# Two expert streams: steps of wide and narrow experts alternate instead of whole experts in turn

## The chip, the cores and the metric

The kernel runs on one core of one Trainium2 chip. The metric is the device time of one execution in microseconds, the median over runs. Arrays are float32; the kernel works on 256 tokens of width 1024.

## The reference

Two layers, each a mixer and then a channel mixer. The first layer's channel mixer is a dense SwiGLU, the second a mixture of eight experts of which each token uses two. The change touches the second alone:

```python
def swiglu(h, w1, w3, w2):
    return (jax.nn.silu(h @ w1) * (h @ w3)) @ w2

def moe_swiglu(h, router_w, w1, w3, w2):
    logits = (h @ router_w).astype(jnp.float32)
    top_v, top_i = lax.top_k(logits, TOP_K)
    probs = jax.nn.softmax(top_v, axis=-1)
    gates = jnp.sum(jax.nn.one_hot(top_i, N_EXPERTS) * probs[..., None], axis=-2)
    y = jnp.zeros_like(h)
    for e in range(N_EXPERTS):
        y = y + gates[..., e:e + 1] * swiglu(h, w1[e], w3[e], w2[e])
    return y
```

Each expert has w1 and w3 of 1024 x 2816 and w2 of 2816 x 1024. After it come `x = x + gt_f * y` and a last RMSNorm with the gains `final_g`.

## The kernel before, in words

The weights of an expert come from HBM in 33 loads of 1 MB (tile `raw`, 128 x 2048): 22 of w1 and w3 (tensors in_m1, in_m3), 11 of w2 (in_m2). `load` (L128) issues them on SP's queue. A tile of `raw` belongs to a pool; in the expert stage there are eight such tiles in turn (`more` and `rawp`, L767 to L771) and, for the first thirteen loads alone, four of a pool `ahead` and one that shares the place of `xn`.

Experts are sorted by how many tokens chose them, into eight places. The even places have 128 slots and are called wide here, the odd ones 64 slots, called narrow. `place` (L843) makes that order on VectorE (DVE): it counts with a matmul, ranks, and writes `number_i`, the expert's number of each place. SP reads seven of these numbers into registers (`values_load`, L878), since a load of any place but the first has its address from such a register (`of_place`, L893). Place 0 is always expert 0.

`prepare` (L905) gathers the tokens of one or two places by matmuls with a one-hot matrix `oh` (tile `pm`, two PSUM banks) and writes `x_hi`, `x_lo` for a wide place (a float32 split into two float32r parts) or `x_n` for a narrow one.

`inner` (L1017) computes one of six column blocks c of w1 and w3; a block is four loads (two for c = 5). For a wide place each half of a load is split by `split` (L133): ScalarE (ACT) writes `whi`, DVE the rest `wlo`, with five pairs of buffers, and PE then takes three matmuls for each product (`mm3`, L152). For a narrow place (`inner_narrow`, L1000) PE multiplies `raw` as it is, in float32, w1 into partitions 0 to 63 and w3 into 64 to 127 of one bank; each such matmul stands as two records in the trace. A narrow block ends with a copy of that bank on ACT (L1014).

`turn` (L971) then transposes the block by four matmuls on PE into a bank `pm` and writes `a_hi`, `a_lo` (wide) or, through Silu on ACT, `a_n` (narrow). `outer` (L1048) multiplies by w2: two banks `pb` for a wide place, one for a narrow place. `scatter` (L1080) splits the result into `ob`, spreads it over the tokens by matmuls with `oht` (bank `pm`) and adds it times the token's gate to `y` on DVE.

The program goes through the places in order (L1117 to L1147): six blocks, then 11 loads of w2. The turn of block c stands behind the matmuls of block c + 1, the scatter of a place behind the first block of the next place. In the third block of the last place, `y` is multiplied by `gate_f` and added to `xs` (L1133, L1134), the gains are loaded over `y` (L1135) and scaled (L1137); the last place's scatter adds to `xs` directly. The queues of the engines are filled in an order that a scheduler finds at build time; each engine then works through its own in that order.

```python
            done = (e, outer(e))
        scatter(*done)
```

Of the kernel before, what the change touches and what calls it, by code (L numbers as in the profile page):

```python
# [17 lines left out]
P = 128  # L18
H = 64
# [18 lines left out]
HOLD_E = (0, 3, 2, 1)  # L38

# [19 lines left out]
def trunk(  # L59
# [49 lines left out]
    def const(shape, dt, name, pl=cst):  # L109
        return pl.tile(shape, dt, tag=name, name=name)  # L110
# [93 lines left out]
    ones = const([P, P], F32, "ones")  # L204
# [179 lines left out]
    def wide(tag):  # L384
        return cst.tile([P, KD, SEQ], F32R, tag=tag, name=nm(tag))
# [371 lines left out]
    def experts():  # L757
# [61 lines left out]
        iota_i = et([P, P], "iota_i", I32)  # L819
        pool.iota(iota_i[:], pattern=[[1, P]], base=1, channel_multiplier=0)  # L820
        iota = et([P, P], "iota")
        dve.tensor_copy(iota[:], iota_i[:])

        def turned(oh, dt):

            tp = pm()
            tv = tp[:, :SEQ].rearrange("p (t s) -> p t s", t=NT)
            for t in range(NT):
                transpose(tv[:, t, :], oh[:, t, :].bitcast(F32))
            o = et([P, NT, P], "oht", dt, bufs=3)  # L830
            act.activation(o[:], tv, AF.Copy)
            return o
# [10 lines left out]
        def place():  # L843
# [60 lines left out]

        def prepare(places):  # L905
# [18 lines left out]
            if e == 0:  # L924

                tn = cst.tile([P, NT, D], F32, tag="wide_lo", name="tn")
# [44 lines left out]
        def turn(p, c, a):  # L971
# [14 lines left out]
            if c == 0 and wide_place(p):  # L986
                for h in ("a_hi", "a_lo"):
                    aa[h] = aa["pool"].tile([P, KF, P], F32R, tag=h, name=nm(h))
            elif c == 0:
                aa["a_n"] = aa["pool"].tile([P, KF, H], F32, tag="a_lo", name=nm("a_n"))  # L990
            if not wide_place(p):
                g = wk.tile([P, 4, H], F32, tag="s", name=nm("g"))
# [55 lines left out]
        def outer(e):  # L1048
            if not wide_place(e):
                acc = pb()  # L1050
                for u in range(11):
# [8 lines left out]
            acc = [pb(), pb()]  # L1060
# [6 lines left out]
            for u in range(11):  # L1067
# [12 lines left out]
        def scatter(e, acc):  # L1080
# [17 lines left out]
            for c in range(2):  # L1098
                s = slice(c * 512, (c + 1) * 512)
                if wide_place(e):  # L1100
                    r = slice(0, P)
                    o_hi, o_lo = parts(c, acc[c][:], gate_f[:, s])
# [13 lines left out]

        prepare((0,))  # L1117
        done = None
        for e in range(NE):
            last = None  # L1120
            for c in range(6):
                a = inner(e, c)
                if c == 0 and done is not None:
                    scatter(*done)
                if last is not None:
                    turn(e, c - 1, last)
                last = a
                if c == 1 and e == 0:
                    place()
                if c == 2 and e == NE - 1:  # L1130
                    y = aa["y"]
                    for t in range(NT):
                        dve.tensor_tensor(y[:, t, :], y[:, t, :], gate_f[:], op=ALU.mult)  # L1133
                        dve.tensor_tensor(xs[:, t, :], xs[:, t, :], y[:, t, :], op=ALU.add)  # L1134
                    act.dma_start(y[:, 0, :], fg.to_broadcast([P, D]))  # L1135
                    fgt = y[:, 1, :]
                    act.activation(fgt, y[:, 0, :], AF.Copy, scale=32.0)  # L1137
                    gn = cst.tile([P, 512], F32, tag="wide_hi", name="gate_n")
                    for i in range(2):
                        r = slice(H * i, H * i + H)  # L1140
                        act.activation(gn[r], gate_f[r, i * 512:(i + 1) * 512], AF.Copy)
                    aa["gate_n"] = gn[:]
            turn(e, 5, last)
            if wide_place(e):
                prepare(tuple(p for p in (e + 1, e + 2) if p < NE))
            done = (e, outer(e))
        scatter(*done)  # L1147

        fin = cst.tile([P, NT, D], F32, tag="wide_lo", name="fin")
# [12 lines left out]
        with tc.If(flag > 0):  # L1162
            for e in range(NE):
# [3 lines left out]
                h = cst.tile([P, KD, P], F32, tag="wide_hi", name=nm("xo"))  # L1167
# [159 lines left out]
```

## Time and profile before

| | us |
|---|---|
| median of 3 runs | 1218.04 (1217.74 to 1220.62) |
| the profiled execution, its own time | 1221.47 |
| its span, first to last instruction | 1219.8 |
| TensorE (PE) busy | 1152.5 (94%) |
| DVE busy | 710.4 (58%) |
| ACT busy | 586.6 (48%) |

A span of 1219.8 us is cut into stages by the trace's time. The first matmul of an expert starts near 483 us, the last near 1201 us, so that the expert stage is 718 us of the span. In it SP issues 264 loads of 1 MB. PE's busy time has modelled ends and is not PE at its peak. Durations below are of this one execution.

### The profile page before, as it was taken

The numbers are of one execution on the slowest core, as the hardware profiler recorded it, in microseconds if no ns is written. First come the engines' busy times: TensorE is split into PE (matmuls) and PEld (weight loads), VectorE is DVE, ScalarE is ACT, GpSimd is POOL, SyncE is SP. The second block draws the span as 40 slices with busy tenths as digits, with TensorE's granted clock in tenths as the row PEclk, the third lists the DMA queues.
The fourth block names the chain that finished last, engine by engine and source line by source line (L and its number), as shares of the span: only waits on it lengthen the run. The fifth ranks groups of instructions, "written<-read, shape, count | busy, mean of one in ns | idle before, by whom it ended". The sixth has DMA issues, their size and how long they took to land. (4 is left out here: it accounts for less than half of the span.)

```text
span 1219.8 us, 16259 instructions
## 1 busy us (share of the span) xinstructions
PE 1152.5 (94%) x6233; PEld 808.1 (66%) x6233; DVE 710.4 (58%) x899; ACT 586.6 (48%) x784; POOL 21.2 (2%) x50
## 2 busy tenths in 40 slices
PE   4899999999999998999998999998999998999994
PEld 2678789998779877887432888333888334787331
DVE  2768646668868556998202889103987104887202
ACT  2664544444347745887112778013777104776101
POOL 1000000000010001000000000000000000000000
PEclk9899999999999997999999999999999999999997
DMA  9976397758966355689799998899999899999893
GB/s 362 391 297 271 126 359 277 279 192 330 356 267 223 128 206 209 244 316 336 302 421 419 420 359 334 339 418 420 419 400 363 316 420 420 420 356 347 351 419 145
DMA packets 57185, 395.72 MB, mean 324 GB/s; under 512 B 8294, under 2 KB 8710, under 8 KB 9356
## 3 DMA queue, kind: packets, MB, share of 16 engines
q1 hardware_dynamic: 54272, 393.24, 82.2%
q10 hardware_dynamic: 2828, 1.37, 0.5%
q8 instruction: 51, 0.84, 0.3%
q14 instruction: 34, 0.28, 0.1%
HBM read 393.53 MB, written 1.05 MB: 323 GB/s over the span
## 5 line engine op out<-in xcount | busy, mean ns | idle before, releaser
L142 DVE TENSOR_TENSOR wlo<-raw,whi 128x1024 fp32r<-128x1024 f32 x386 | 459.2, 1220 | 106.4 <-ACT whi L141 104.4
L141 ACT ACTIVATE whi<-raw 128x1024 fp32r<-128x1024 f32 x386 | 395.9, 1059 | 184.6 <-PE pa L403 87.6
L1011 PE MATMUL pa<-raw,x_n 128*64 128x512 f32 (+1 forms) x768 | 173.5, 561 | 0.0
L402 PE MATMUL pa<-wide_hi,whi 128*128 128x256 f32 x544 | 153.4, 283 | 0.2 <-DVE wide_hi L376 0.2
L403 PE MATMUL pa<-wide_lo,whi 128*128 128x256 f32 x544 | 152.6, 281 | 0.2 <-DVE wide_lo L377 0.2
L404 PE MATMUL pa<-wide_hi,wlo 128*128 128x256 f32 x544 | 152.6, 281 | 0.0
L154 PE MATMUL pa<-wlo,x_hi 128*128 128x512 f32 (+1 forms) x384 | 149.4, 389 | 1.3 <-DVE wlo L142 1.0
L155 PE MATMUL pa<-whi,x_lo 128*128 128x512 f32 (+1 forms) x384 | 146.0, 381 | 0.0
L153 PE MATMUL pa<-whi,x_hi 128*128 128x512 f32 (+1 forms) x384 | 144.4, 384 | 0.0
L1011 PEld LDWEIGHTS pa<-raw,x_n 128*64 128x64 f32 x768 | 55.2, 136 | 93.3 <-issue 89.2
L402 PEld LDWEIGHTS pa<-wide_hi,whi 128*128 128x128 f32 x544 | 102.2, 188 | 6.4 <-issue 4.0
L403 PEld LDWEIGHTS pa<-wide_lo,whi 128*128 128x128 f32 x544 | 102.4, 188 | 1.5 <-issue 1.1
L404 PEld LDWEIGHTS pa<-wide_hi,wlo 128*128 128x128 f32 x544 | 102.4, 188 | 0.3 <-issue 0.3
L1056 PE MATMUL pb<-raw,a_n 128*64 128x512 f32 x352 | 85.1, 601 | 15.4 <-DMA raw<-in_m_dram 14.2
L1014 ACT ACTIVATE s<-pa 128x512 f32<-128x512 f32 (+1 forms) x24 | 13.5, 561 | 167.7 <-PE pa L1011 167.7
L994 DVE TENSOR_TENSOR a_n<-g,pm 128x256 f32<-128x256 f32 (+1 forms) x24 | 9.6, 399 | 142.0 <-ACT g L993 142.0
L154 PE MATMUL pb<-wlo,a_hi 128*128 128x512 f32 x220 | 87.3, 398 | 0.0
L154 PEld LDWEIGHTS pa<-wlo,x_hi 128*128 128x128 f32 x384 | 73.2, 191 | 20.5 <-DVE wlo L142 7.0
L155 PE MATMUL pb<-whi,a_lo 128*128 128x512 f32 x220 | 86.0, 392 | 0.0
L153 PEld LDWEIGHTS pa<-whi,x_hi 128*128 128x128 f32 x384 | 73.2, 191 | 16.8 <-issue 1.8
L155 PEld LDWEIGHTS pa<-whi,x_lo 128*128 128x128 f32 x384 | 73.4, 191 | 13.6
L153 PE MATMUL pb<-whi,a_hi 128*128 128x512 f32 x220 | 74.3, 395 | 0.0
(312 smaller groups left out, 1284.0 us busy)
## 6 DMA issues: line engine op xcount, KB each, us to landing
raw<-in_m_dram SPq DMA_DIRECT2D x264, 1024.0 KB, 9.2
raw<-in_ada_w_dram SPq DMA_DIRECT2D x48, 1024.0 KB, 7.4
raw<-in_f_dram SPq DMA_DIRECT2D x33, 1024.0 KB, 5.8
raw<-in_win_dram SPq DMA_DIRECT2D x20, 1024.0 KB, 5.4
raw<-in_wout_dram SPq DMA_DIRECT2D x8, 1024.0 KB, 6.1
xs<-in_x_dram SPq DMA_DIRECT2D x1, 1024.0 KB
out_dram<-fin SPq DMA_DIRECT2D x2, 512.0 KB, 4.0
y<-in_fg_dram ACTq DMA_DIRECT2D x1, 512.0 KB, 7.1
```

The costliest lines, as they stand in the source:

```text
L141: act.activation(hi[:, :n], src, AF.Copy)
L142: dve.tensor_tensor(lo[:, :n], src, hi[:, :n].bitcast(F32), op=ALU.subtract)
L153: pe.matmul(ps, l_hi, r_hi, start=first, stop=False)
L154: pe.matmul(ps, l_hi, r_lo, start=False, stop=False)
L155: return pe.matmul(ps, l_lo, r_hi, start=False, stop=last)
L402: pe.matmul(pv[:, b, :], wh, h_hi[:, k, :], start=(k == 0), stop=False)
L403: pe.matmul(pv[:, b, :], wh, h_lo[:, k, :], start=False, stop=False)
L404: pe.matmul(pv[:, b, :], wl, h_hi[:, k, :], start=False, stop=(k == KD - 1))
L994: dve.tensor_tensor(aa["a_n"][:, o, :], g[:, :n, :], tv[:, :n, H:], op=ALU.mult)
L1011: pe.matmul(ps[H * i:H * i + H, :n], x_n[:, k, :], w[:, kk * n:(kk + 1) * n], start=(k == 0), stop=(k == KD - 1))
L1014: act.activation(a[:, :n], ps[:, :n], AF.Copy)
L1056: pe.matmul(acc[H * c:H * c + H, :], aa["a_n"][:, k, :], w[:, i * 1024 + c * 512:i * 1024 + (c + 1) * 512], start=(k == 0), stop=(k == KF ...
```

## The change

The eight places become two streams: places 0, 2, 4, 6 (wide) and 1, 3, 5, 7 (narrow). A step is one block of `inner` with its turn (4 loads, 2 for c = 5), or four, four and three loads of `outer`; a place has nine steps. The first twelve steps go by the string 000101101101 (0 is a wide step), and from there on wide and narrow steps alternate. What ends a step (turn, scatter, and so on) is written behind the matmuls of the next step. `outer` of a narrow place accumulates in a bank of the pool `pa` over its three steps. `values_load` moves from `place` to the first load of a place other than 0. The work on `y`, `xs` and the gains (`last_gate`) moves behind the scatter of place 6. Several tiles get their own places in SBUF (`x_hi`, `x_lo`, `a_n` as `big`, a fourth `oht`).

```diff
+FIRST_TURNS = "000101101101"
...
-            for p in range(1, NE):
-                ids[p] = nc.values_load(number_i[0:1, p:p + 1], engines=(mybir.EngineType.SP,), min_val=0,
-                                        max_val=NE - 1)
+            placed["number"] = number_i
...
         def of_place(w_, p, u):
 
+            if p and not ids:
+                for q in range(1, NE):
+                    ids[q] = nc.values_load(placed["number"][0:1, q:q + 1], engines=(mybir.EngineType.SP,),
+                                            min_val=0, max_val=NE - 1)
...
             if hi_ > P:
-                x_hi = cst.tile([P, KD, P], F32R, tag="wide_hi", name=nm("x_hi"))
-                x_lo = cst.tile([P, KD, P], F32R, tag="wide_lo", name=nm("x_lo"))
+                x_hi, x_lo = et([P, KD, P], "x_hi", F32R), et([P, KD, P], "x_lo", F32R)
...
-        def outer(e):
+        def outer(e, units, acc):
+
             if not wide_place(e):
-                acc = pb()
-                for u in range(11):
+                acc = acc or pa()
+                for u in units:
...
+        def last_gate():
+
+            y = aa["y"]
+            for t in range(NT):
+                dve.tensor_tensor(y[:, t, :], y[:, t, :], gate_f[:], op=ALU.mult)
+                dve.tensor_tensor(xs[:, t, :], xs[:, t, :], y[:, t, :], op=ALU.add)
+            act.dma_start(y[:, 0, :], fg.to_broadcast([P, D]))
+            act.activation(y[:, 1, :], y[:, 0, :], AF.Copy, scale=32.0)
...
+        def steps(p):
+
+            for c in range(6):
+                a = inner(p, c)
+
+                def rest_of(c=c, a=a):
+                    turn(p, c, a)
+                    if p == 0 and c == 0:
+                        place()
+                    if p == 0 and c == 1:
+                        prepare((1,))
+                    if c == 5 and not wide_place(p) and p + 2 < NE:
+                        prepare((p + 2, p + 1))
+                yield rest_of
+            acc = None
+            for units in ((0, 1, 2, 3), (4, 5, 6, 7), (8, 9, 10)):
+                acc = outer(p, units, acc)
+
+                def rest_of(u=units[-1], acc=acc):
+                    if u == 10:
+                        scatter(p, acc)
+                        if p == NE - 2:
+                            last_gate()
+                yield rest_of
...
+        streams = [all_steps(range(i, NE, 2)) for i in range(2)]
+        left_over = None
+        for i in map(int, FIRST_TURNS + "01" * (9 * NE // 2 - 6)):
+            rest_of = next(streams[i])
+            if left_over:
+                left_over()
+            left_over = rest_of
+        left_over()
```

How the built program's order moves is shown at three places. The first is SP's queue at the start of the stage; `number_i` is the table of experts' numbers, L130 and L131 are the loads. Before, behind the first twelve loads:

```order
L130 DMA raw632_4539<-in_m3_dram 128x2048
L130 DMA raw707_4890<-in_m1_dram 128x2048
L130 DMA raw712_4912<-in_m3_dram 128x2048
...
L130 DMA raw755_5090<-in_m1_dram 128x2048
L878 TENSOR_LOAD number_i672_4693
L878 ISA x2
...
L130 DMA raw760_5124<-in_m3_dram 128x2048
```

and with the change:

```order
L131 DMA raw633_4539<-in_m3_dram 128x2048
L896 TENSOR_LOAD number_i673_4693
L896 ISA x2
...
L131 ISA
L131 DMA raw715_4942<-in_m1_dram 128x2048
L131 ISA
L131 DMA raw716_4944<-in_m3_dram 128x2048
```

The seven reads of `number_i` stood behind load 21 and stand behind load 12 now; no load passes them.

The second is ACT's queue in the blocks of a pair of places. `whi` are halves of wide loads, L997 and L998 write `a_hi`, L1044 and L1045 are the wide block's Silu. Before, inside a wide place:

```order
L1044 ACTIVATE s955_5994<-pa933_5904 128x512
L141 ACTIVATE whi967_6032<-raw966_6030 128x1024
L141 ACTIVATE whi969_6042<-raw966_6030 128x1024
L141 ACTIVATE whi972_6054<-raw971_6052 128x1024
L141 ACTIVATE whi974_6064<-raw971_6052 128x1024
L997 ACTIVATE a_hi957_6002<-pm982_6099 128x512
L141 ACTIVATE whi977_6076<-raw976_6074 128x1024
```

and with the change, where L1015 is the copy that ends a narrow block:

```order
L1045 ACTIVATE s1006_6219<-pa984_6129 128x512
L994 ACTIVATE g1008_6227<-pm1007_6222 128x256
L998 ACTIVATE a_hi949_5989<-pm1015_6257 128x512
L142 ACTIVATE whi1019_6268<-raw1018_6266 128x1024
L1015 ACTIVATE s1014_6255<-pa1009_6230 128x512
L142 ACTIVATE whi1021_6278<-raw1018_6266 128x1024
L142 ACTIVATE whi1024_6290<-raw1023_6288 128x1024
L142 ACTIVATE whi1026_6300<-raw1023_6288 128x1024
```

One of the eight halves of the next wide block stands ahead of the narrow block's copy, seven behind it.

The third is PE's queue in the same blocks. L1011 and L1012 are narrow matmuls, L154 to L156 wide ones, L222 and L223 transposes. Before, between two narrow blocks:

```order
L1011 MATMUL pa1408_7983<-raw1411_7996,x_n1327_7616 64x512
L1011 MATMUL pa1408_7983<-raw1412_7998,x_n1327_7616 64x512
L1011 MATMUL pa1417_8019<-raw1418_8020,x_n1327_7616 64x512
L222 MATMUL pm1423_8046<-ident_82,s1413_8008 128x128 x4
L1011 MATMUL pa1417_8019<-raw1419_8022,x_n1327_7616 64x512
```

and with the change, at a narrow block's start and at its end:

```order
L154 MATMUL pa985_6130<-whi1004_6209,x_hi847_5526 128x512
L1012 MATMUL pa1009_6230<-raw1010_6231,x_n849_5528 64x512
L155 MATMUL pa985_6130<-wlo1005_6210,x_hi847_5526 128x512
...
L156 MATMUL pa985_6130<-whi1004_6209,x_lo848_5527 128x512
L1012 MATMUL pa1009_6230<-raw1011_6233,x_n849_5528 64x512
...
L223 MATMUL pm1015_6257<-ident_82,s1006_6219 128x128 x4
L1012 MATMUL pa1009_6230<-raw1012_6243,x_n849_5528 64x512
...
L1012 MATMUL pa1009_6230<-raw1013_6245,x_n849_5528 64x512
L154 MATMUL pa1016_6264<-whi1019_6268,x_hi847_5526 128x512
L223 MATMUL pm1039_6357<-ident_82,s1014_6255 128x128 x4
```

A narrow block of 16 matmuls is cut into one, which stands alone five matmuls before the wide block's end, seven, the wide block's transposes, and eight; one wide matmul and the narrow block's transposes follow.

## Rows read from the trace of the kernel before

**Rows 1.** Stretches: us, busy us (instructions) of each engine, PE clock, DMA share, GB/s.
```profile
661.00:769.00 108.00, 106.63 (x497) 83.88 (x495) 90.71 (x97) 78.59 (x99) 0.00 (x0) 0.98 0.96 377
769.00:841.00 72.00, 65.87 (x306) 22.52 (x302) 5.96 (x12) 5.02 (x12) 0.00 (x0) 1.00 0.95 387
850.00:905.00 55.00, 55.00 (x247) 44.00 (x246) 48.89 (x48) 41.28 (x47) 0.00 (x0) 1.00 1.01 419
```
**Rows 2.** Timeline of PE: first scatter of the first and the last narrow place.
```profile
662.20 0.73 PE L1108 MATMUL pm<-ob,oht 64*128 64x512 f32 x2 [0.69 <-ACT ob L1092]
...
1202.79 0.73 PE L1108 MATMUL pm<-ob,oht 64*128 64x512 f32 x2 [1.45 <-ACT ob L1092]
```
**Rows 3.** Timeline of PE: matmuls of two successive w2 loads of a narrow place.
```profile
1196.83 1.94 PE L1056 MATMUL pb<-raw,a_n 128*64 128x512 f32 x8 [0.45 <-SPq L1162]
...
1199.40 1.94 PE L1056 MATMUL pb<-raw,a_n 128*64 128x512 f32 x8 [0.63 <-SPq L1162]
```
**Rows 4.** Timeline of PE inside a wide block.
```profile
860.16 0.39 PE L153 MATMUL pa<-whi,x_hi 128*128 128x512 f32 x1
...
861.79 0.40 PE L154 MATMUL pa<-wlo,x_hi 128*128 128x512 f32 x1
```
**Rows 5.** Timeline of PE over two narrow blocks.
```profile
780.28 7.09 PE L1011 MATMUL pa<-raw,x_n 128*64 128x512 f32 x32
788.05 0.66 PE L222 MATMUL pm<-ident,s 128*128 128x128 f32 x4 [0.68 <-ACT s L1014]
788.64 7.09 PE L1011 MATMUL pa<-raw,x_n 128*64 128x512 f32 x32
```
**Rows 6.** Timeline of PE where a narrow place's first matmuls stand among wide ones.
```profile
765.64 0.39 PE L153 MATMUL pb<-whi,a_hi 128*128 128x512 f32 x1
765.96 1.07 PE L1011 MATMUL pa<-raw,x_n 128*64 128x512 f32 x2
766.96 0.50 PE L154 MATMUL pb<-wlo,a_hi 128*128 128x512 f32 x1
767.30 0.39 PE L155 MATMUL pb<-whi,a_lo 128*128 128x512 f32 x1
...
768.09 3.65 PE L1011 MATMUL pa<-raw,x_n 128*64 128x512 f32 x14
771.66 0.50 PE L1108 MATMUL pm<-ob,oht 128*128 128x512 f32 x1
```
**Rows 7.** The page's costliest groups, of ACT and DVE.
```profile
L142 DVE TENSOR_TENSOR wlo<-raw,whi 128x1024 fp32r<-128x1024 f32 x386 | 459.2, 1220 | 106.4 <-ACT whi L141 104.4
L141 ACT ACTIVATE whi<-raw 128x1024 fp32r<-128x1024 f32 x386 | 395.9, 1059 | 184.6 <-PE pa L403 87.6
...
L1014 ACT ACTIVATE s<-pa 128x512 f32<-128x512 f32 (+1 forms) x24 | 13.5, 561 | 167.7 <-PE pa L1011 167.7
```
**Rows 8.** Stretches at the start of the stage; columns as in rows 1.
```profile
480.00:495.00 15.00, 15.00 (x63) 12.76 (x62) 11.18 (x17) 10.37 (x17) 0.00 (x0) 0.73 0.06 25
495.00:522.00 27.00, 27.00 (x123) 21.83 (x122) 25.26 (x41) 22.91 (x25) 0.00 (x0) 1.00 0.81 311
```
**Rows 9.** Timeline of DVE, and the instructions that read `number_i`: durations ns, first and last start.
```profile
518.23 0.17 DVE L876 CAST number_i<-number 128x8 int32<-128x8 f32 x1
...
L878 SPq TENSOR_LOAD <-number_i x7: 261/263/472, 518.4 to 522.1; - x7
```
**Rows 10.** Timeline of DVE at the end.
```profile
1204.05 1.41 DVE L1115 SCALAR_TENSOR_TENSOR xs<-pm,gates_p,xs 128x512 f32<-128x512 f32 x2 [0.59 <-PE pm L1109]
...
1210.66 1.28 DVE L1156 SCALAR_TENSOR_TENSOR fin<-xs,rs,y 128x1024 f32<-128x1024 f32 x1 [0.66 <-POOL rs L341]
```
**Rows 11.** Groups of lines L1115, L1133, L1134: durations ns min/median/max; the page's DMA issue.
```profile
L1115 DVE SCALAR_TENSOR_TENSOR y<-pm,gates_p,y x24: 743/750/752, 663.5 to 1137.8; 128x512 f32<-128x512 f32 x24
L1133 DVE TENSOR_TENSOR y<-y,gate_f x2: 1226/1226/1226, 1134.3 to 1138.6; 128x1024 f32<-128x1024 f32 x2
L1134 DVE TENSOR_TENSOR xs<-xs,y x2: 1224/1225/1226, 1135.6 to 1139.8; 128x1024 f32<-128x1024 f32 x2
...
y<-in_fg_dram ACTq DMA_DIRECT2D x1, 512.0 KB, 7.1
```

More of the change, by code (lines that the diff above doesn't have):

```diff
@@ L202, in trunk @@
     dve.tensor_scalar(nspc[:], s_[:], -8.0, None, op0=ALU.mult)
-    ones = const([P, P], F32, "ones")
+    ones = const([P, P], F32, "ones", pre)
     pool.memset(ones[:], 1.0)
@@ L384, in wide @@
     def wide(tag):
-        return cst.tile([P, KD, SEQ], F32R, tag=tag, name=nm(tag))
+        return pre.tile([P, KD, SEQ], F32R, tag=tag, name=nm(tag))
     def load_fill(ap, n):
@@ L816, in experts @@
         dve.scalar_tensor_tensor(pos[:], pv, 1.0, sel[:], op0=ALU.add, op1=ALU.mult)
-        iota_i = et([P, P], "iota_i", I32)
-        pool.iota(iota_i[:], pattern=[[1, P]], base=1, channel_multiplier=0)
+        iota_i = et([P, 2, P], "h32", I32, bufs=2)[:, 0, :]
+        pool.iota(iota_i, pattern=[[1, P]], base=1, channel_multiplier=0)
         iota = et([P, P], "iota")
-        dve.tensor_copy(iota[:], iota_i[:])
+        dve.tensor_copy(iota[:], iota_i)
         def turned(oh, dt):
@@ L829, in turned @@
                 transpose(tv[:, t, :], oh[:, t, :].bitcast(F32))
-            o = et([P, NT, P], "oht", dt, bufs=3)
+            o = et([P, NT, P], "oht", dt, bufs=4)
             act.activation(o[:], tv, AF.Copy)
@@ L924, in prepare @@
             if e == 0:
-                tn = cst.tile([P, NT, D], F32, tag="wide_lo", name="tn")
+                tn = et([P, NT, D], "big")
                 for t in range(NT):
@@ L988, in turn @@
                     aa[h] = aa["pool"].tile([P, KF, P], F32R, tag=h, name=nm(h))
-            elif c == 0:
-                aa["a_n"] = aa["pool"].tile([P, KF, H], F32, tag="a_lo", name=nm("a_n"))
             if not wide_place(p):
+                if c == 0:
+                    aa["a_n"] = et([P, KF, H], "big")
                 g = wk.tile([P, 4, H], F32, tag="s", name=nm("g"))
@@ L1059, in outer @@
                 return acc
-            acc = [pb(), pb()]
+            acc = acc or [pb(), pb()]
             def add(k, part, c):
@@ L1065, in add @@
                     k == 0, k == KF - 1)
-            for u in range(11):
+            for u in units:
                 w = load(of_place(m2, e, u))
@@ L1101, in scatter @@
                     r = slice(0, P)
-                    o_hi, o_lo = parts(c, acc[c][:], gate_f[:, s])
+                    o_hi, o_lo = parts(c, acc[c][:], None)
                 else:
@@ L1115, in scatter @@
                         dve.scalar_tensor_tensor(dst[:, t, s], sp[:], gcol, dst[:, t, s], op0=ALU.mult, op1=ALU.add)
-        prepare((0,))
[L1118 to L1146, printed above, removed]
@@ L1147, in experts @@
-        scatter(*done)
-        fin = cst.tile([P, NT, D], F32, tag="wide_lo", name="fin")
+        def last_gate():
[5 more added lines that the diff above has]
+            act.activation(y[:, 1, :], y[:, 0, :], AF.Copy, scale=32.0)
+            gn = et([P, 512], "x_n")
+            for i in range(2):
+                r = slice(H * i, H * i + H)
+                act.activation(gn[r], gate_f[r, i * 512:(i + 1) * 512], AF.Copy)
+            aa["gate_n"] = gn[:]
@@ new lines, in all_steps @@
+        def all_steps(places):
+            for p in places:
+                yield from steps(p)
+        prepare((0,))
+        streams = [all_steps(range(i, NE, 2)) for i in range(2)]
[6 more added lines that the diff above has]
+        left_over()
+        fgt = aa["y"][:, 1, :]
+        fin = et([P, NT, D], "big")
@@ L1166, in experts @@
                     dve.tensor_scalar(oh[:, t, :], iota[:], placed["past"][:, t, e:e + 1], None, op0=ALU.is_equal)
-                h = cst.tile([P, KD, P], F32, tag="wide_hi", name=nm("xo"))
+                h = et([P, KD, P], "x_hi")
                 for q in range(2):
```

## The prediction

> **What bounds the kernel now.** The expert stage decides, since the change leaves the rest as it was. I read first the stretches by stage. While PE works on a wide place it is never short of work: in the middle of one it is busy for 55.00 of 55 us, and the transfers run at 419 GB/s beside it; over a whole wide place they fall to 377 GB/s. While it works on a narrow place, 72 us, PE is busy for 65.87 us and the transfers give 387 GB/s [rows 1]. So neither side is full all the time, and that is what the change goes for. From the first to the last narrow scatter are three pairs of places in 540.6 us [rows 2], 180.2 us for a pair. The transfers alone would need less: 66 loads of 1.049 MB at 420 GB/s (2.5 us each) are 165 us. The reader should then look at what a pair costs PE, because that is the other floor.
>
> Wide: consecutive matmuls start 0.233 us apart (seven steps in 1.63 us) [rows 4]. A block of 48 takes 11.2 us, with the four transposes, 0.59 us between two runs [rows 5], 11.8 us. Narrow: 32 records, 16 matmuls, take 7.09 us with their end, 0.43 us each, and one block follows the other after 8.36 us; the transposes wait 0.68 us for ACT's copy [rows 5]. In the second half of a narrow place eight records (four matmuls) need 4 x 0.43 = 1.72 us and the next load's start 2.57 us later [rows 3]: here PE does wait for transfers, 0.85 us on seven of the eleven loads, some 6 us in a narrow place. This and what the scatters cost is all that better overlap can give back.
>
> **The change part by part**, against the profiled execution (1221.47 us, span 1219.8).
>
> *The blocks.* Five times in a pair a wide and a narrow block change places with each other. Before they cost 11.8 + 8.4 = 20.2 us. Now PE's order cuts the narrow block. One matmul stands alone among wide ones. The trace has this case once: two wide matmuls with a lone narrow one between take 767.30 - 765.64 = 1.66 us [rows 6]; less 2 x 0.23 for the wide ones it costs 1.20 us, where a matmul in a run costs 0.43. Two narrow matmuls run side by side in the two halves of the array, and the lone one has no partner. Then come seven, 771.66 - 768.09 = 3.57 us [rows 6], the wide block's transposes 0.59, eight matmuls 3.44 and 0.2 for leaving, and the narrow block's own transposes 0.59. With the wide matmuls that is 11.2 + 1.20 + 3.57 + 0.59 + 3.64 + 0.59 = 20.8 us.
>
> To this come two waits. The transposes still wait for ACT's copy; one wide matmul fills 0.23 of the 0.68 us [rows 5], so 0.45 remain. And behind the copy stand seven of the next wide block's eight halves in ACT's queue, so the second half is begun only after the copy. ACT 0.60 + 1.06 and DVE 1.22 us [rows 5, 7] make 2.9 us after the narrow block's end, while PE has the wait, the transposes and six wide matmuls to do, 2.65 us: 0.3 us more. The block pair comes to 21.5 us, 1.3 more than before, and above the transfers' 20.0 us (8 x 2.5). Five of them cost 6.5 us more, the half-sized sixth about 1.4 (the cutting there is no cheaper than half).
>
> What rows show of ACT is that it stands idle for 167.7 us before these copies [rows 7]; they do not show whether work behind a waiting copy could pass it. The Trainium skill (PSUM — Partial Sum Buffer, Engine vs sequencer instructions) says that the queues of ScalarE and VectorE are strict first-in, first-out. By that rule the seven halves must wait, as I assume; if they could pass, the second wait would go, 0.3 us x 20 blocks, and the sum below would be 6 us less.
>
> *The w2 steps.* A narrow step is entered twice (four matmuls, then twelve, among wide ones); I take 0.3 us for entering and leaving, a little over the 0.2 us by which the lone matmul's 1.20 exceeds its own 1.00 (765.96 to 766.96) [rows 6]: three steps, 2 us. Against that, the waits for loads (6 us) go [rows 3], since wide work fills them. The scatters now stand among other matmuls: PE waited 0.69 us before the first [rows 2], and a scatter cut a narrow run [rows 6]; I put this at 4 us, between nothing and the 9 us that 16 such matmuls and the cuts take now beyond wide work. A pair: +6.5 + 1.4 + 2 - 6 - 4, about zero; with what an order with two streams in it adds that I cannot see, +1 us, between -6 and +8.
>
> *The start.* `number_i` is written at 518.23 us and SP's seven reads end at 522.6 [rows 9]. Before, eight more loads had moved by then: 311 GB/s over 27 us are 8.4 MB [rows 8]. Now none of them may go before the reads. PE has three wide blocks in hand from 483 us, 36 us with the first gather, and is done at about 520, the gather for place 1 (32 matmuls) to 524. In the new DVE order `number_i` stands one `wlo` earlier, so I take 521.6 for the first load, 4 to 5 us to its landing (between the 2.5 us of its transfer and the 7.1 us of the gains' load) [rows 11], and from there the 32 loads of the first rounds at 2.5 us, 80 us: the sixth blocks of both places end near 609 us. Their w2 steps (132 x 0.233 = 30.8, 44 x 0.43 = 18.9, gathers 3.6, entering 2, transposes and the first scatter 2) end at about 666 us, where before the last narrow matmul of place 1 ended at 661.5 (662.20 less the wait of 0.69) [rows 2]: +5 us (0 to +10).
>
> *The pairs.* Two more at +1, and the last one without a gather behind it, -3: last matmul of an expert +4 us.
>
> *The end.* Before, `y` had been folded into `xs` 60 us ahead; DVE's first addition to `xs` came 3.3 us after the last weights' matmul and the last `fin` started at 1210.66 [rows 10]. Now between the last wide scatter and the narrow one stand, on DVE alone, four additions (0.75 each), four full-width operations (1.23 each) and three parts of `ob` and `o` (0.69): 10 us [rows 11], of which the last narrow matmuls (5 us) hide half. Behind them the gains are loaded, 7.1 us to landing [rows 11], or, an estimate, 4 to 5 with idle queues, then scaled on ACT, with three squares queued behind. DVE's four additions and the norm hide part. +6 us (+4 to +9).
>
> **Sum.** +5 + 2 - 3 + 6 = +10 us: 1231.5 us on the profiled execution. The median of the runs is 3.4 us under that execution, so 1228.
>
> **The rivals.**
>
> *The transfers take over (faster).* If the cutting costs nothing (the lone matmul and the seven hide beside wide work) and the copies do not hold ACT up, a pair of blocks is at most 20.0 us and a pair of places 165 to 168 us. For it: DVE and ACT are busy for 85% and 73% in a wide place, so there is room [rows 1]. Against it: the lone matmul has its price in the trace, on the same engine among the same neighbours [rows 6]. The point from which it decides is a block pair of 20.0 us. Three pairs at -13 and the same start and end: 1228 - 42 = 1186. Halfway, with the waits gone but the cutting paid (0.75 us x 20), 1213.
>
> *Nothing to measure.* The start costs nothing because the first rounds catch up, and the gains' load hides: 1228 - 9 = 1219.
>
> *Waits pile up (much slower).* Each of the three engines works in a fixed order made of two streams; if each block pair waits for DMA or for `wlo` once more, 23 us, the sum rises by 1.5 x 20 = 30 us to 1258. For it: wide places already show 1.4 us of PE idle each [rows 1]. Against it: loads run ahead, with eight tiles for eight loads in 21.5 us.
>
> That the streams would not alternate in the built program is excluded by the order.
>
> **How the numbers follow.** Chances: my forecast 0.55, with a range of its own from 1220 to 1238 (the start's and the end's bounds and a pair's +-3); faster by the transfers' way, in full 0.07 and in part 0.15; nothing to measure 0.13; piled-up waits 0.10. From 1202 to 1246 the range leaves out the full takeover and most of the pile-up. About 0.3% (3.7 us) is what a measurement of this kernel tells from no change: faster than 1214.4 has 0.20 (takeover, and most of the part), same 0.19 (nothing to measure, and the edges of the forecast and of the part), slower 0.61.
>
> **What would show it.** Right: block pairs 21 to 22 us apart in the timeline; in it lone narrow matmuls of 1.07 us and idle time before the transposes put down to the copy; transfers under 420 GB/s in all rounds after the first; a gap in the transfers from about 480 to 522 us; a last w2 matmul a little after 1201 us and at least 24 us from there to the end. Wrong: block pairs of 20.0 us with transfers at 420 GB/s and PE waiting for DMA (then the cutting was overpriced), or 23 us with idle time before `wlo`.

## The result, and the profile after

The changed kernel takes 1229.04 us (median of 7 runs, 1228.77 to 1229.83), beside 1218.68 us for the kernel before on the same chip: a ratio of 1.0076 (95% interval 1.0058 to 1.0094). It is slower by 0.8%; 1228.0 us were predicted. The profiled execution has a span of 1228.1 us, 8.3 us more than before. The difference of the medians is larger, 10.4 us, because the profiled execution of the kernel before was slow for its kernel: 1221.47 us, 2.8 us above this median, where that of the changed kernel is 0.8 us above its own.

Below, a pair is a wide place and the narrow place behind it (place 2 and place 3, say), and a block pair is one block of each.

**The start.** Stretches of the profile after, columns as in [rows 1]:

```profile
480.00:495.00 15.00, 15.00 (x64) 12.70 (x64) 11.28 (x16) 10.51 (x16) 0.00 (x0) 0.76 0.00 1
495.00:522.00 27.00, 26.99 (x135) 22.52 (x133) 23.58 (x48) 18.48 (x24) 0.00 (x0) 1.00 0.02 3
522.00:545.00 23.00, 20.21 (x82) 9.98 (x82) 8.13 (x11) 9.44 (x15) 0.00 (x0) 0.85 1.00 416
```

Where 311 GB/s moved between 495 and 522 us before [rows 8], 3 GB/s move now. PE then stands idle for 2.79 of 23 us, and the granted clock of that stretch is 0.85 on average.

**The pairs.** Instructions of the narrow places' w2 line, place by place: count, ns min/median/max, first and last start. First the kernel before, then the changed one:

```profile
L1056 PE MATMUL pb<-raw,a_n x88: 592/592/644, 635.8 to 660.9; 128*64 128x512 f32 x88
L1056 PE MATMUL pb<-raw,a_n x88: 592/592/643, 816.8 to 840.9; 128*64 128x512 f32 x88
L1056 PE MATMUL pb<-raw,a_n x88: 592/592/643, 994.8 to 1020.1; 128*64 128x512 f32 x88
L1056 PE MATMUL pb<-raw,a_n x88: 592/592/644, 1175.9 to 1200.8; 128*64 128x512 f32 x88
```

```profile
L1058 PE MATMUL pa<-raw,big x88: 592/593/644, 622.7 to 667.3; 128*64 128x512 f32 x88
L1058 PE MATMUL pa<-raw,big x88: 592/592/644, 803.4 to 847.7; 128*64 128x512 f32 x88
L1058 PE MATMUL pa<-raw,big x88: 592/592/644, 984.8 to 1028.2; 128*64 128x512 f32 x88
L1058 PE MATMUL pa<-raw,big x88: 592/592/644, 1162.6 to 1204.3; 128*64 128x512 f32 x88
```

From the last starts: place 1 ends 6.4 us later (667.3 against 660.9). The three pairs behind it, each from the last w2 matmul of one narrow place to that of the next, take 180.4, 180.5 and 176.1 us (before 180.0, 179.2 and 180.7). From the last w2 matmul to the end of the span are 23.8 us (before 19.0). 6.4 + 0.4 + 1.3 - 4.6 + 4.8 = 8.3 us.

**A block pair.** Timeline of PE, place 3's narrow blocks between place 2's wide ones:

```profile
703.68 0.40 PE L154 MATMUL pa<-whi,x_hi 128*128 128x512 f32 x1
704.00 1.07 PE L1012 MATMUL pa<-raw,x_n 128*64 128x512 f32 x2
705.01 0.50 PE L155 MATMUL pa<-wlo,x_hi 128*128 128x512 f32 x1
...
706.37 3.65 PE L1012 MATMUL pa<-raw,x_n 128*64 128x512 f32 x14
709.94 0.66 PE L223 MATMUL pm<-ident,s 128*128 128x128 f32 x4
710.53 3.65 PE L1012 MATMUL pa<-raw,x_n 128*64 128x512 f32 x16
714.11 0.51 PE L154 MATMUL pa<-whi,x_hi 128*128 128x512 f32 x1
714.91 0.66 PE L223 MATMUL pm<-ident,s 128*128 128x128 f32 x4 [0.29 <-ACT s L1015]
...
716.56 0.40 PE L154 MATMUL pa<-whi,x_hi 128*128 128x512 f32 x1
717.11 0.51 PE L155 MATMUL pa<-wlo,x_hi 128*128 128x512 f32 x1 [0.16 <-DVE wlo L143]
...
731.51 0.66 PE L223 MATMUL pm<-ident,s 128*128 128x128 f32 x4
```

One narrow matmul (two records) takes 1.00 us of PE's time alone, 704.00 to 705.01; then come seven, then eight. The transposes at 714.91 start 0.80 us after the wide matmul ahead of them, where the instruction behind such a first wide matmul usually starts after 0.34 (705.01 to 705.35): 0.46 us of waiting for ACT's copy. At 717.11 another 0.32 us go to `wlo` (0.55 less the usual 0.23). From one wide block's transposes to the next (709.94 to 731.51) it is 21.57 us.

What stands behind the two waits is seen on ACT, one block pair later:

```profile
732.70 1.05 ACT L142 ACTIVATE whi<-raw 128x1024 fp32r<-128x1024 f32 x1
735.82 0.60 ACT L1015 ACTIVATE s<-pa 128x512 f32<-128x512 f32 x1 [2.08 <-PE pa L1012]
736.32 6.73 ACT L142 ACTIVATE whi<-raw 128x1024 fp32r<-128x1024 f32 x7
```

ACT does one wide half, stands idle for 2.08 us until the narrow block's last matmul lets it copy, and only then does the other seven halves.

**The end.** DVE, the last rows:

```profile
1206.90 1.21 DVE L1123 TENSOR_TENSOR y<-y,gate_f 128x1024 f32<-128x1024 f32 x1
1208.03 0.68 DVE L1095 TENSOR_TENSOR ob<-o,ob 128x512 fp32r<-128x512 f32 x1
1208.63 1.22 DVE L1123 TENSOR_TENSOR y<-y,gate_f 128x1024 f32<-128x1024 f32 x1
1209.77 2.35 DVE L1124 TENSOR_TENSOR xs<-xs,y 128x1024 f32<-128x1024 f32 x2
1212.04 1.40 DVE L1117 SCALAR_TENSOR_TENSOR xs<-pm,gates_p,xs 128x512 f32<-128x512 f32 x2
...
1219.32 1.28 DVE L1181 SCALAR_TENSOR_TENSOR big<-xs,rs,y 128x1024 f32<-128x1024 f32 x1 [0.66 <-POOL rs L342]
```

`last_gate` (L1123, L1124) runs from 1206.90 to 1212.1, behind the last w2 matmul at 1204.3. The last `fin` (here the tile `big` of L1181) starts 15.0 us after that matmul, where before it was 9.9 (1210.66 [rows 10] less 1200.8).

### The profile page after: what moved, and what is told of

The parts are those of the page before. It is cut to its first block, busy times and chain, and to the rows that moved or that the text cites. A ratio compares the mean times of both kernels' runs of the same rounds, so it can differ in the third digit from the quotient of the medians.

```text
span 1228.1 us, 16215 instructions
## 1 busy us (share of the span) xinstructions
PE 1171.9 (95%) x6233; PEld 804.6 (66%) x6233; DVE 713.8 (58%) x899; ACT 582.3 (47%) x784; POOL 20.6 (2%) x50
## 5 line engine op out<-in xcount | busy, mean ns | idle before, releaser
L143 DVE TENSOR_TENSOR wlo<-raw,whi 128x1024 fp32r<-128x1024 f32 x386 | 458.3, 1221 | 206.4 <-ACT whi L142 203.1
L142 ACT ACTIVATE whi<-raw 128x1024 fp32r<-128x1024 f32 x386 | 391.1, 1054 | 239.5 <-PE pa L404 88.9
L1012 PE MATMUL pa<-raw,x_n 128*64 128x512 f32 (+1 forms) x768 | 187.5, 570 | 1.1 <-DMA raw<-in_m_dram 1.0
L154 PE MATMUL pa<-whi,x_hi 128*128 128x512 f32 (+1 forms) x384 | 146.8, 384 | 0.0
L156 PE MATMUL pa<-whi,x_lo 128*128 128x512 f32 (+1 forms) x384 | 144.0, 376 | 0.0
L1012 PEld LDWEIGHTS pa<-raw,x_n 128*64 128x64 f32 x768 | 56.6, 138 | 97.4 <-issue 87.1
L154 PEld LDWEIGHTS pa<-whi,x_hi 128*128 128x128 f32 x384 | 72.7, 189 | 28.3 <-issue 12.9
L156 PE MATMUL pb<-whi,a_lo 128*128 128x512 f32 x220 | 86.1, 392 | 0.0
L1058 PE MATMUL pa<-raw,big 128*64 128x512 f32 x352 | 84.7, 601 | 0.0
L156 PEld LDWEIGHTS pa<-whi,x_lo 128*128 128x128 f32 x384 | 72.9, 190 | 11.6
L154 PE MATMUL pb<-whi,a_hi 128*128 128x512 f32 x220 | 74.3, 401 | 0.0
L998 ACT ACTIVATE a_hi<-pm 128x512 fp32r<-128x512 f32 (+1 forms) x24 | 13.4, 560 | 118.7 <-PE pm L223 118.6
L999 DVE TENSOR_TENSOR a_lo<-pm,a_hi 128x512 fp32r<-128x512 f32 (+1 forms) x24 | 15.5, 647 | 72.4 <-ACT a_hi L998 72.4
```

Source lines behind the costliest of these rows:

```text
L142: act.activation(hi[:, :n], src, AF.Copy)
L143: dve.tensor_tensor(lo[:, :n], src, hi[:, :n].bitcast(F32), op=ALU.subtract)
L154: pe.matmul(ps, l_hi, r_hi, start=first, stop=False)
L156: return pe.matmul(ps, l_lo, r_hi, start=False, stop=last)
L998: act.activation(a_hi[:, o, :], tv[:, :n, :], AF.Copy)
L999: dve.tensor_tensor(a_lo[:, o, :], tv[:, :n, :], a_hi[:, o, :].bitcast(F32), op=ALU.subtract)
```

## The experiments

The median of the kernel before is 1217.4 to 1219.2 us, depending on the set of runs; each ratio is to that of its own set.

| run | what it is | us | ratio (95% interval) |
|---|---|---|---|
| e1_whole | change, places whole in turn | 1202.14 | 0.9856 (0.9826 to 0.9885) |
| e5_prep | e1_whole, `prepare` where it was before | 1216.55 | 0.9975 (0.9958 to 0.9993) |
| e8_before | before, `prepare` where the change has it | 1206.18 | 0.9916 (0.9890 to 0.9942) |
| e2_pair | change, narrow blocks not cut | 1210.60 | 0.9928 (0.9900 to 0.9956) |
| e9_late | change, narrow transposes later | 1229.88 | 1.0093 (1.0077 to 1.0110) |
| e11_ahead | e9_late, copy later too | 1216.84 | 0.9990 (0.9973 to 1.0006) |
| e3_tail | change, `last_gate` earlier | 1224.89 | 1.0042 (1.0027 to 1.0057) |
| e4_start | change, four wide steps first | 1224.26 | 1.0042 (1.0028 to 1.0056) |
| e6_combo | edits of e2_pair, e3_tail, e4_start | 1195.13 | 0.9813 (0.9784 to 0.9842) |
| e7_pair0 | edits of e2_pair, e3_tail; first two places whole | 1195.69 | 0.9819 (0.9789 to 0.9849) |
| e10_cover | e6_combo, DVE's product covered | 1184.61 | 0.9723 (0.9707 to 0.9739) |
| e12_early | e10_cover, `number_i` early | 1184.01 | 0.9726 (0.9700 to 0.9752) |

### Is it the alternation? (e1_whole, e5_prep, e8_before)

e1_whole undoes the alternation and nothing else:

```diff
-        for i in map(int, FIRST_TURNS + "01" * (9 * NE // 2 - 6)):
+        for i in map(int, ("0" * 9 + "1" * 9) * (NE // 2)):
```

> The changed kernel with its tiles and code, but the steps of a place in one piece: place 0 whole, then place 1 whole, and so on; the alternation alone is undone. Theory (the +10 us come from the first reads of number_i, from cut narrow blocks and from last_gate behind place 6's last step): all three go, since nine wide steps stand ahead of the first narrow load and last_gate comes some 70 us before the end; 1218 to 1221 us, as the kernel before, scatters 180 us apart. Rival (the new sharing of tiles and banks costs, whatever the order): 1224 to 1229 us, with scatters over 181.5 us apart.

It took 1202.14 us: less than the changed kernel and less than the kernel before, and below the ranges of the theory and of the rival. So the alternation as built costs 27 us, and the change holds something else that gains. The candidate was `prepare`, which the diff moves from behind a wide place's sixth block to behind a narrow place's. e5_prep moves it back in e1_whole, e8_before moves it alone in the kernel before:

```diff
-                    if p == 0 and c == 1:
-                        prepare((1,))
-                    if c == 5 and not wide_place(p) and p + 2 < NE:
-                        prepare((p + 2, p + 1))
+                    if c == 5 and wide_place(p):
+                        prepare(tuple(q for q in (p + 1, p + 2) if q < NE))
```

> As e1_whole (places whole, one after the other), but prepare for the next two places is called where the kernel before had it, behind a wide place's sixth block, in place of behind a narrow place's sixth block. Theory (what made e1_whole 17 us faster than the kernel before is that the gathers and the making of x_hi, x_lo and x_n moved out of the wide places, where PE is the limit, into the narrow ones, where PE waits for transfers): 1215 to 1221 us, scatters 179 to 181 us apart. Rival (something else in the new code does it, such as the banks of the narrow accumulation or the tiles): 1200 to 1206 us.

```diff
+                if c == 2 and e == 0:
+                    prepare((1,))
...
-            if wide_place(e):
-                prepare(tuple(p for p in (e + 1, e + 2) if p < NE))
+            if not wide_place(e) and e + 2 < NE:
+                prepare((e + 2, e + 1))
```

> The kernel before with one thing of the change: prepare((e + 2, e + 1)) behind the sixth block of a narrow place e, and prepare((1,)) behind the second block of place 0, in place of both behind the sixth block of a wide place. Theory (as for e5_prep): 1200 to 1206 us, scatters 174 to 176 us apart. Rival (it needs the rest of the new code too): 1214 to 1220 us.

e5_prep came out by the theory, 1216.55 us (1215 to 1221), and so did e8_before but for 0.2 us, 1206.18 us (1200 to 1206). A wide and a narrow place, of e5_prep and then of e1_whole, as stretches:

```profile
658.00:763.00 105.00, 103.42 (x487) 82.45 (x484) 89.99 (x95) 77.43 (x97) 0.00 (x0) 0.98 0.96 380
763.00:838.00 75.00, 68.91 (x314) 23.71 (x314) 6.59 (x12) 6.10 (x14) 0.00 (x0) 1.00 0.94 384
```

```profile
657.00:757.30 100.30, 98.74 (x448) 78.39 (x446) 86.45 (x83) 72.54 (x79) 0.00 (x0) 0.98 0.99 396
757.30:832.80 75.50, 71.87 (x351) 27.88 (x350) 10.26 (x24) 12.24 (x32) 0.00 (x0) 1.00 0.95 390
```

The wide place loses 39 of PE's instructions and 4.7 us; the narrow place takes 37 in (68.91 to 71.87 us busy) and grows by 0.5 us only, since PE waited for loads there. In this pair that is 4.2 us, and it needs no alternation. (The profiled execution of e5_prep, 1220.86 us, is the longest of its ten, so that the two traces lie 18 us apart and the medians 14.4.)

The waits themselves can be read as well: what PE waited for in all, over the pair behind place 1 (us in total, times, longest). Loads, in the kernel before and in e1_whole; then the scatters' wait for `ob`, in the kernel before and in the changed kernel:

```profile
PE pb L1056 <- DMA raw<-in_m_dram: 3.4, 6, 0.6
PE pa L1058 <- DMA raw<-in_m_dram: 0.2, 1, 0.2
```

```profile
PE pm L1108 <- ACT ob L1092: 0.7, 1, 0.7
PE pm L1110 <- ACT ob L1094: 0.5, 1, 0.5
```

e5_prep has the 3.4 us on loads again, e8_before has none in this pair, and the changed kernel has none. So moving `prepare` alone ends these waits, and alternating the steps does not have to. The last pair, in which nothing is gathered, is the exception: e8_before has 3.4 us of them there, the changed kernel none.

### What is in a block pair (e2_pair, e9_late, e11_ahead)

```diff
-                    for i, w in enumerate((w1, w3)):
+                    for i, w in ((1, w3), (0, w1)):
                         pe.matmul(ps[H * i:H * i + H, :n], x_n[:, k, :], w[:, kk * n:(kk + 1) * n],
```

> The changed kernel with one edit: in a narrow block the w3 matmul of each k stands ahead of the w1 matmul. As the w3 load is issued behind the w1 load, no narrow matmul can be ordered alone among wide ones, and the built order has all 16 of a block in one run, then 7 wide ones, the narrow block's transposes, 41 wide ones and the wide block's transposes, now straight behind the matmuls that they depend on. Theory (the broken pair and the entering of a run three times cost PE 1.4 us in a block pair, and 0.45 us go with the copy's wait, against some 0.9 us of a new wait for DVE's product): block pairs of 20.3 to 20.8 us in place of 21.57, 20 of them: 1205 to 1214 us. Rival (transfers or free buffers set the 21.57 us, and the cut fills time that is there anyway): block pairs of 21.3 to 21.6 us, 1226 to 1230 us.

1210.60 us, as the theory said; block pairs of 20.10 us, 0.2 us under its range. The rows of PE show both sides of the trade:

```profile
713.95 0.60 PE L223 MATMUL pm<-ident,s 128*128 128x128 f32 x4
...
734.05 0.60 PE L223 MATMUL pm<-ident,s 128*128 128x128 f32 x4
...
744.84 0.66 PE L223 MATMUL pm<-ident,s 128*128 128x128 f32 x4 [0.78 <-DVE s L1046]
745.42 7.09 PE L1012 MATMUL pa<-raw,x_n 128*64 128x512 f32 x32
```

All 16 matmuls stand in one run of 7.09 us and the copy's wait is gone, but PE waits 0.78 us for DVE's product. e9_late leaves the cuts and moves the narrow block's transposes only:

```diff
+                if not wide_place(p) and recent:
+                    order.enter_context(tc.issue_after(recent[1].ins))
                 for b in range(n):
                     transpose(tv[:, b, :], a[:, b * P:(b + 1) * P])
```

> The changed kernel with one edit: a narrow block's transposes may go only behind the sixth matmul of the next wide block, where they went behind its first; the cuts of the narrow block and ACT's order (one wide half, the copy, seven halves) stay. Theory (ACT takes its queue in order, so the copy delays the second half, and that chain, copy 0.60, half 1.06, wlo 1.22 us behind the narrow block's end, is what PE waits for in the end): the 0.45 us before the transposes turn up before the first matmul that needs the second wlo, block pairs stay between 21.3 and 21.6 us, 1224 to 1230 us. Rival (the two waits are separate, or a half passes the copy): block pairs of 21.1 us or less, 1216 to 1221 us.

1229.88 us, and block pairs of 21.57 us, as in the changed kernel. The wait before the transposes is gone, and stands whole at the second `wlo`:

```profile
737.25 0.60 PE L223 MATMUL pm<-ident,s 128*128 128x128 f32 x4
737.60 0.47 PE L154 MATMUL pa<-whi,x_hi 128*128 128x512 f32 x1
738.76 0.50 PE L155 MATMUL pa<-wlo,x_hi 128*128 128x512 f32 x1 [0.68 <-DVE wlo L143]
```

So it is one chain, copy, second half, `wlo`. e11_ahead takes the copy out from between the halves, to behind the last of them:

```diff
-            a = wk.tile([P, 512], F32, tag="s", name=nm("s"))
-            act.activation(a[:, :n], ps[:, :n], AF.Copy)
-            return a
+            return ps
...
+                    with ExitStack() as behind:
+                        if recent:
+                            behind.enter_context(tc.issue_after(halves[1].ins))
+                        act.activation(a[:, :m], ps[:, :m], AF.Copy)
```

> As e9_late, and the copy of a narrow block is made with its transposes, so that it stands behind all eight halves of the next wide block in ACT's queue and the transposes go behind the next narrow block's first matmul; the cuts stay (1, 7 and 8 matmuls). Theory (both waits hang on the copy's place in ACT's queue; the rest above 20 us is the cutting): block pairs of 20.7 to 20.9 us, 1211 to 1217 us. Rival (the waits are not what it costs, or come back before the wide block's product): block pairs of 21.3 us or more, 1224 to 1230 us; rival of the other side (the waits were all, and the cuts cost nothing): 20.1 us, 1205 to 1209 us.

1216.84 us, at the upper edge of the theory's range; block pairs are shorter than it said:

```profile
708.96 0.66 PE L224 MATMUL pm<-ident,s 128*128 128x128 f32 x4
...
723.18 1.07 PE L1024 MATMUL pa<-raw,x_n 128*64 128x512 f32 x2
724.18 0.66 PE L224 MATMUL pm<-ident,s 128*128 128x128 f32 x4
...
729.50 0.66 PE L224 MATMUL pm<-ident,s 128*128 128x128 f32 x4
```

20.54 us from 708.96 to 729.50, with the cuts still there. 1.03 us went, 0.25 more than the 0.78 of waits. In part that may be that the narrow transposes now stand straight behind the lone matmul, so that PE breaks off its wide matmuls once less; it was not measured apart.

### The end and the start (e3_tail, e4_start)

```diff
-            last = e == NE - 1
+            last = e >= NE - 2
...
-                        if p == NE - 2:
+                        if p == NE - 3:
                             last_gate()
```

Beside it, place 6's `ob` takes the gate (`gate_f[:, s]` in place of `None`), and `gate_n` is made behind place 7's sixth block, when its tile is free.

> The changed kernel with last_gate behind place 5's scatter, some 180 us earlier; places 6 and 7 both add to xs with the gate in their ob. Theory (the folding of y and the load of the gains stand on the path at the end): the end from the last w2 matmul goes from 23.8 us back to about 19, 1223 to 1225 us. Rival (the additions hide behind the last narrow matmuls and the gains' load behind the norm; the end is longer because two scatters meet there): 1228 to 1230 us, with 23 us or more from the last w2 matmul to the end.

1224.89 us. Place 5's last w2 matmul starts at 1027.3, place 7's at 1201.3, and the span ends at 1223.1. From place 5 to the end it is 195.8 us in place of 199.9, but only 2.0 of these 4.1 us lie behind the last w2 matmul (21.8 us in place of 23.8; the theory said 19): the rest came in the last pair. The other 2.8 us, down to the 19.0 of the kernel before, speak for the rival, that two scatters meet at the end: in e3_tail the last matmuls of place 6's scatter start at 1204.61 us, 3.3 us behind the last w2 matmul, and place 7's scatter follows them. In e1_whole, where `last_gate` stands behind place 6's scatter as in the changed kernel but place 7 lies whole in between, the end is 18.7 us.

```diff
-FIRST_TURNS = "000101101101"
+FIRST_TURNS = "000010110111"
```

> The changed kernel with four wide steps ahead of the first narrow one (turns 0000 10 11 01 11 in place of 000 1 0 11 0 11 01), so that four more loads of place 0 go out before SP reads number_i. Theory (the gap in the transfers up to 522 us costs about 5 us): the last narrow matmul of place 1 comes 4 to 9 us earlier than at 667 us, and the run takes 1220 to 1225 us. Rival (PE has so much to catch up in the first two places that the gap hides): 1228 to 1230 us, last narrow matmul of place 1 at 666 us or later.

1224.26 us; place 1's last w2 matmul at 659.3 us, 8.0 earlier. Stretches:

```profile
495.00:522.00 27.00, 27.00 (x125) 22.18 (x124) 25.82 (x42) 22.66 (x26) 0.00 (x0) 1.00 0.34 120
522.00:545.00 23.00, 23.00 (x117) 14.48 (x116) 11.98 (x25) 10.81 (x19) 0.00 (x0) 1.00 0.99 409
```

PE no longer stands between 522 and 545 us, and its clock stays at 1.00. The edit also thins out the alternation in the first two places and leaves part of the gap (120 GB/s, where the kernel before has 311), so the 8.0 us are not the price of the gap alone. In the medians 4.8 us are left.

### Putting them together (e6_combo, e7_pair0, e10_cover, e12_early)

e6_combo is the edits of e2_pair, e3_tail and e4_start together.

> The changed kernel with the edits of e2_pair, e3_tail and e4_start together. Theory (three separate places on the path: 18.4, 4.1 and 4.8 us less): 1199 to 1204 us. Rival (with block pairs at 20.1 us, which is what eight transfers need, the transfers are the limit and the start has nothing to give): 1205 to 1209 us.

1195.13 us, 4 us below the theory's range: the three edits gave 18.4, 4.1 and 4.8 us alone, 27.3 in sum, and give 33.9 together. The start is worth more beside uncut blocks: place 1 ends at 655.9 us, 11.0 earlier than in e2_pair (666.9), where the edit alone gave 8.0.

e7_pair0 keeps e2's and e3's edits and changes the order of the steps:

```diff
-        for i in map(int, FIRST_TURNS + "01" * (9 * NE // 2 - 6)):
+        for i in map(int, "0" * 9 + "1" * 9 + "01" * (9 * (NE // 2 - 1))):
```

> e2_pair and e3_tail together, but places 0 and 1 whole, one after the other as in e1_whole, and the streams alternate only from places 2 and 3 on. Theory (up to the end of place 1 nothing but loading ahead counts, which whole places do best; last narrow matmul of place 1 at 657 us as in e1_whole, then pairs of 173.4, 173.2 and 168.9 us as in e2_pair and 20 us to the end): 1189 to 1196 us. Rival (what e1_whole does up to 657 us leaves less of place 2 loaded, so the pair behind it is longer by that): 1197 to 1203 us.

1195.69 us, near the upper end of the theory's range and within 0.6 us of e6_combo: with the blocks uncut, it makes hardly a difference whether the first two places alternate. e10_cover takes e6_combo and covers the wait for DVE's product:

```diff
+                if wide_place(p) and recent:
+                    order.enter_context(tc.issue_after(recent[7].ins))
                 for b in range(n):
                     transpose(tv[:, b, :], a[:, b * P:(b + 1) * P])
```

> As e6_combo, but a wide block's transposes go behind the eighth matmul of the next narrow block, so that DVE's product (0.78 us of wait on PE in e2_pair) is covered. Theory (block pairs of 20.1 us are the transfers' own pace, eight loads of 2.5 us): PE's wait is only moved to the loads, block pairs of 20.0 to 20.1 us, 1193 to 1196 us. Rival (PE's order still sets the pace): block pairs of 19.3 us, some 16 of them, 1181 to 1186 us.

The theory fell: 1184.61 us, within the rival's 1181 to 1186. Rows of PE, and stretches of 100 us and one block pair:

```profile
696.82 0.66 PE L223 MATMUL pm<-ident,s 128*128 128x128 f32 x4
...
716.22 0.66 PE L223 MATMUL pm<-ident,s 128*128 128x128 f32 x4
```

```profile
660.00:760.00 100.00, 99.77 (x447) 60.21 (x448) 59.44 (x61) 47.04 (x59) 0.00 (x0) 1.00 1.01 413
690.00:709.60 19.60, 19.60 (x91) 12.02 (x90) 11.26 (x12) 9.64 (x12) 0.00 (x0) 1.00 1.02 421
```

Block pairs of 19.40 us, with PE full. Eight loads of 1.049 MB in 19.40 us are 432 GB/s; the transfers run at 421. The difference, some 0.5 us of transfers per block pair, can come only from loads that went ahead; over a whole pair of places, 170.0 us (826.3 less 656.3), 66 loads need 407 GB/s.

```diff
+        place()
         prepare((0,))
...
-                    if p == 0 and c == 0:
-                        place()
```

> As e10_cover, but place() is called ahead of prepare((0,)), so that number_i stands behind 7 products wlo in DVE's order since the making of t_lo, in place of 25, and should be written near 487 us, where e10_cover wrote it at 516.5. Theory (SP's reads of number_i hold the loads back, and with the matmuls of a place in uncut runs each load that goes earlier counts): 117 GB/s between 495 and 522 us become over 300, the last narrow matmul of place 1 comes 3 to 10 us before 656.3 us, and the run takes 1175 to 1182 us. Rival (the loads wait for free tiles there, or PE is the limit of the first two places): 1183 to 1187 us.

`number_i` came at 485.8 us and the transfers did as the theory said, but the time lay with the rival: 1184.01 us, 0.6 us under e10_cover. Stretches as in e4_start:

```profile
495.00:522.00 27.00, 27.00 (x127) 21.95 (x125) 23.98 (x29) 22.75 (x27) 0.00 (x0) 1.00 0.83 311
522.00:545.00 23.00, 23.00 (x120) 15.57 (x119) 14.03 (x18) 13.40 (x21) 0.00 (x0) 1.00 0.71 259
```

The gap is filled, the transfers then slow down further on, and PE, which had work all along, ends place 1 only 1.6 us earlier (654.7 against 656.3).

## Why the prediction was right, and where it was not

- **Block pair, 21.5 us predicted: 21.57.** Its terms hold as well. The waits read from the rows are 0.46 + 0.32 = 0.78 us (0.75 predicted), and what is left, 20.8, is the predicted sum with the cuts. Against e10_cover's 19.40, where no narrow run is cut and nothing waits, the cutting costs 1.4 us.
- **ACT's queue.** The assumption that the halves cannot pass the waiting copy holds: ACT idles for 2.08 us with them behind it, and e9_late and e11_ahead show that only the copy's place counts. The rule of the Trainium skill (PSUM — Partial Sum Buffer, Engine vs sequencer instructions), strict first-in, first-out, agrees. But the two waits are not two costs, as the sum had them: they are one chain, and taking away the first alone gave nothing (e9_late).
- **The transfers as a floor: wrong.** The rival's point of decision, a block pair of 20.0 us, is no floor. e10_cover passes it; loads that went ahead make up for it. What can be a floor is the time of a whole pair's transfers, 165 us, and e10_cover's three pairs, at 170.0, 170.6 and 165.0 us, stay at or above it.
- **The pair, +1 us predicted: +0.4 and +1.3.** The size is right and its reason is not. The step that failed is the one on the w2 steps, -6 for the waits for loads and -4 for the scatters, both put down to the alternation. The diff moves `prepare` from the place where PE is full into the one where PE waits, and I gave that move no term of its own. By e1_whole and e5_prep it gains 14.4 us in all, by e8_before 13.0 against the kernel before, and by the waits shown there it ends PE's waiting for loads, but for the last pair, without any alternation. (Both figures are of whole places; among alternating steps the place of `prepare` was not tested.) The -4 had no row behind it beyond the wait of 0.69 us, and little came: PE's wait for `ob` went from 0.7 to 0.5 us. On the other side the alternation as built costs 27 us over the same tiles: by the traces of e1_whole and the changed kernel, 10.5 us until place 1 is done, 11.5 over the three pairs and 5.1 at the end. So the forecast of +10 us came out because a gain that had no term and a cost that was set too low cancelled, and that is luck. The alternation does give something back once its steps are not cut: the pair behind place 1 takes 175.7 us in e1_whole, 173.6 in e2_pair and 170.0 in e10_cover.
- **The start, +5 us (0 to +10): +6.4.** The reads ended at 520.3 us, the first narrow matmul began at 525.5, and the gap in the transfers is there. e4_start and e12_early narrow the reason down: with four wide steps first, PE has no idle time between 495 and 545 us though most of the gap is left, and filling the rest of it (e12_early) changes the time by 0.6 us. So the gap costs where three wide steps, with their loads, are too little work for PE to reach across it. How the 6.4 us divide between PE's 2.79 us of idle time, its lower clock from 525 to 530 us and what follows was not measured.
- **The last pair, -3: -4.6 against the pair before. The end, +6 (+4 to +9): +4.8.** Of the 4.8, `last_gate` (the operations on DVE, and the gains that ACT scales at 1214.66 us, 3.6 us after their load was issued) holds for less than half: moving it gives 2.0 us behind the last w2 matmul (e3_tail; 2.1 more come in the last pair). The other 2.8 stay, most likely with the two scatters that meet.
- **Sum, +10 us: +8.3 on the profiled execution, +10.4 between the medians.** That the median came within some 1 us is in part luck too: the profiled execution took 1229.83 us, 1.7 under the 1231.5, but the 3.4 us taken off for the median are 0.8 for this kernel. The pile-up of waits and the transfers' takeover did not happen in this kernel. e10_cover's 1184.61 us lies beside the takeover's 1186, but by another way: PE is full there, its pairs with a gather take 170 us and not 165 to 168, and the start and the end are mended too, which the takeover left as they were.

## What to carry to other kernels

When two streams are interleaved, read from the built order where the finer of them is cut: an instruction that only runs cheaply beside its partner must not be parted from it, and here the order of two matmuls against that of their loads decided that. In an engine that takes its queue in order, an instruction that waits for the other stream delays all that stands behind it, so move the waiting instruction and not its consumer. And undo one part of a change at a time, since a gain elsewhere in the diff can hide what the headline part costs: here 13.0 us were to be had in the kernel before with four lines (e8_before). The alternation did not pay as built, nor with uncut blocks alone (e2_pair, 8.5 us behind e1_whole); it paid once the start and the end were mended as well (e6_combo, 7.0 us ahead of it).

## What the runs showed of the hardware

- Two narrow fp32 matmuls in the two halves of the array take 0.86 us together (0.43 each in a run), and one alone takes 1.00 us; parting one pair costs 2 x 1.00 - 0.86 = 1.14 us, most of the 1.4 us of the cutting.
- Loads that stood ready let a stretch of blocks draw 432 GB/s worth of tiles while the transfers ran at 417 to 421 GB/s (e10_cover, 690.0 to 729.2 us); 27 us at 117 in place of 311 GB/s (e10_cover beside e12_early) moved the end by 0.6 us.
- Between 522 and 545 us the changed kernel's granted clock was 0.85 on average, where e4_start, with no idle PE there, had 1.00. Within it, PE stood idle for 0.45 us before the transposes at 524.25 and for 0.44 before the first narrow matmul, at 525.49; from 525 to 530 us the clock was 0.50, the lower of its two levels (1.2 GHz). The two records of that first matmul took 1.97 us, where a lone one takes 1.07 at the full clock.
